# Storing a quarter of two heads through GpSimd's DMA queue

## The chip, the cores and the metric

The kernel runs on one core of a Trainium2 chip. The core has compute engines (PE for matmuls, VectorE or DVE, ScalarE or ACT, GpSimd or POOL), a queue engine SP, and 16 DMA engines that move data between HBM (the chip's DRAM) and SBUF (on-chip memory with 128 partitions). [...] DMAs are issued by SP, ACT or GpSimd; each issuer has a queue of its own, and all queues run on the same 16 DMA engines. The metric is device time in microseconds (us); lower is better.

## The reference

```python
# q, k: (8, 12, 1024, 64) float32
def reference(q, k):
    return np.einsum('bhid,bhjd->bhij', q, k).astype(np.float32)
```

For each of the 96 heads a 1024 x 64 matrix is multiplied with the transpose of another: 1024 x 1024 scores of 4 bytes, 4 MB for a head, 402.65 MB written in all, against 50.33 MB read.

## The kernel before, in words

The 96 heads are worked in blocks of 2, 2, 4, 8, 8 and then six times 12. Inputs of a block are loaded by `load` (L66, ACT's queue from the second load on), cast to fp16 by GpSimd (L127), and transposed by VectorE (L145) into `qT` and `kT`. This runs a block or two ahead; in the last block, heads 84 to 95, nothing is left to load, cast or transpose.

`scores` (L156) makes one head. PE multiplies (L171) into PSUM in four pieces of 128 x 2048; ScalarE copies each piece into the head's output tile `o_sb` (L181); then SP issues one store of the whole tile (L185). In `o_sb` a partition holds eight rows of the head's result (index t, 0 to 7), each 1024 floats, and partition p holds rows 8p to 8p + 7; so what one partition stores is one run of 32 KB in HBM, and the head is 128 such runs.

`out_pool` (L45) has three buffers. The first copy into `o_sb` for head n + 3 therefore waits for the store of head n to land, all of it. All instructions are held in the order in which they are written (`pin`), on each engine; what runs when is decided by that order and by the waits on semaphores.

A DMA reports its end through a semaphore, to which the DMA engines that took part add their marks. The kernel's DMAs take their semaphores in turn out of eight for each kind of queue, so a DMA also waits for the landing of the one that stood eight before it.

Of the kernel before, what the change touches and what calls it, by code (L numbers as in the profile page):

```python
# [10 lines left out]
P = 128  # L11

@with_exitstack
def kernel(
# [6 lines left out]
    nc = tc.nc  # L21

    B, H, S, D = q.shape
    NT = S // P
    BH = B * H
# [5 lines left out]
    of = out.rearrange("b h i j -> (b h) i j")  # L31
# [3 lines left out]
    PE_BLOCKS = 2  # L35
    NMAX = max(sizes)
    CHUNK = 48 * 32

    consts = ctx.enter_context(tc.tile_pool(name="consts", bufs=1))
    ident = consts.tile([P, P], F16)  # L40
# [4 lines left out]
    out_pool = ctx.enter_context(tc.tile_pool(name="out_pool", bufs=3))  # L45

    pin = tc.keep_in_program_order

    def half_tile():
        half_sb = half_pool.tile([P, CHUNK], F16, tag="half")  # L50
        return half_sb

    class Block:
# [3 lines left out]
        def __init__(self, first, N, by_pe):  # L57
# [5 lines left out]
            self.halves = {}  # L63
            self.cut = max(1, self.R * 32 // CHUNK + (self.R * 32 % CHUNK > 0))

# [90 lines left out]
        def scores(self, n, side, ps_pool, w):  # L156

            half, g = divmod(n, self.N // 2)
            cs = slice(half * D, (half + 1) * D)

            qT = self.qT.rearrange("c (g m t) -> c g t m", t=NT, m=P)
            kT = self.kT.rearrange("c (g j) -> c g j", j=S)
            o_sb = out_pool.tile([P, NT, S], F32, tag="out")
            for u in range(NT // w):
                ps = ps_pool.tile([P, w * S], F32, tag="po")
                for tt in range(w):
                    for j in range(2):
                        js = slice(j * 512, (j + 1) * 512)
                        at = tt * S + j * 512
                        pin(  # L170
                            nc.tensor.matmul(  # L171
                                ps[:, at : at + 512],
                                qT[cs, g, w * u + tt],
                                kT[cs, g, js],
                            )
                        )
                dst = o_sb[:, w * u : w * u + w].rearrange("p t j -> p (t j)")
                if w == 1 and u % 2:
                    pin(nc.vector.tensor_copy(out=dst, in_=ps))  # L179
                else:  # L180
                    pin(nc.scalar.copy(out=dst, in_=ps))  # L181
                for do in side.get(u, []):
                    do()
            pin(
                nc.sync.dma_start(  # L185
                    out=of[self.first + n].rearrange("(p t) j -> p (t j)", p=P),
                    in_=o_sb.rearrange("p t j -> p (t j)"),
                )
            )

    blocks, first = [], 0
    for i, N in enumerate(sizes):
# [5 lines left out]
    at = 0  # L198
# [110 lines left out]
```

## Time and profile before

| | |
|---|---|
| median of three runs | 1063.38 us (1062.9 to 1063.62) |
| span of the profiled execution, first to last instruction | 1061.8 us |
| HBM traffic over the span | 427 GB/s |
| stores, issue to landing, median of 96 | 21.8 us |
| copies PSUM to `o_sb`, L181 (ScalarE) | 695.3 us in 384 instructions, mean 1.86 us |
| ScalarE waiting for a store to land | 298.4 us |
| DMA instructions of GpSimd | none |

Only the span is given for the profiled execution; the median of the runs is 1.6 us above it, and that difference lies before its first and behind its last instruction. A busy time is the time in which an engine had an instruction at work. "DMA share" is the mean busy share of the 16 DMA engines. In the chain of waits, each line names what was waited for, with its start and duration. An engine name with a q (SPq, ACTq) is the queue side, where DMAs are issued.

### The profile page before, as it was taken

Reading aid. Unit: us, or ns where it says so; the run is one execution under the profiler, and the core shown is the slowest. Engines: PE = TensorE matmul, PEld = TensorE weight load, DVE = VectorE, ACT = ScalarE, POOL = GpSimd, SP = SyncE. Lnnn points to the kernel's source line nnn. Section 1 sums busy time; section 2 is a strip of 40 time slices with the busy share of each in tenths; the row PEclk is TensorE's granted clock in tenths of the full one; section 3 lists DMA queues with packets and bytes.
Section 4 is the critical chain, followed back from the end, with each engine's and each line's share of the span. In section 5 each row is a group of like instructions: output and inputs, shape, how many; then the busy total and the mean of one; then the engine's idle time right before and its main releaser. Section 6 shows DMA issues by size and latency. Waiting matters only on the chain.

```text
span 1061.8 us, 4282 instructions
## 1 busy us (share of the span) xinstructions
PE 701.3 (66%) x1568; PEld 241.6 (23%) x1568; DVE 471.5 (44%) x75; ACT 697.6 (66%) x386; POOL 368.3 (35%) x286
## 2 busy tenths in 40 slices
PE   6866755755677367773677836777367777778770
PEld 2322211211222122221222212222122222222220
DVE  2999601991696007960079600795007950000000
ACT  4856745755777366774677746777467777777771
POOL 6959128607630463303733046330463200000000
DMA  9999999999999999999999999999999999999997
GB/s 385 428 429 435 433 431 435 435 422 440 428 430 432 432 430 432 435 422 429 431 433 431 415 436 431 433 435 422 428 434 435 434 432 432 434 433 427 434 431 311
DMA packets 17588, 453.25 MB, mean 427 GB/s; under 512 B 1952, under 2 KB 1952, under 8 KB 2976
## 3 DMA queue, kind: packets, MB, share of 16 engines
q1 hardware_dynamic: 14688, 406.85, 89.1%
q10 hardware_dynamic: 2880, 46.14, 10.4%
q8 instruction: 12, 0.20, 0.1%
q14 instruction: 8, 0.07, 0.0%
HBM read 50.33 MB, written 402.65 MB: 427 GB/s over the span
## 4 chain that ended last, share of the span: by engine, by line
DMA 70%; ACT 17%; PE 7%; DVE 2%; issue 1%; POOL 1%; ACTq 0%; SPq 0%
DMA out_dram<-o_sb 70%; ACT o_sb L181 17%; PE ps L171 7%; DVE qT L145 1%; DVE kT L145 1%; DMA early<-in_q_dram 0%; POOL half_sb L127 0%; PE ps L151 0%; POOL half_sb L97 0%; DVE kT L154 0%; DVE o_sb L179 0%; ACTq L181 0%; ACT kT L154 0%; SPq L84 0%; ACTq L73 0%
## 5 line engine op out<-in xcount | busy, mean ns | idle before, releaser
L181 ACT COPY o_sb<-ps 128x2048 f32<-128x2048 f32 (+1 forms) x384 | 695.3, 1860 | 334.7 <-DMA out_dram<-o_sb 298.4
L171 PE MATMUL ps<-kT,qT 64*128 64x512 f16 x1536 | 697.2, 617 | 329.4 <-ACT o_sb L181 325.6
L127 POOL CAST half_sb<-x_sb 32x1536 f16<-32x1536 f32 (+1 forms) x256 | 346.5, 1353 | 455.1 <-DMA x_sb<-in_q_dram 318.3
L171 PEld LDWEIGHTS <-qT 64*128 64x128 f16 x1536 | 238.4, 157 | 786.3 <-issue 781.9
L145 DVE STREAM_TRANSPOSE qT<-half_sb 128x1536 f16<-128x1536 f16 (+1 forms) x34 | 232.8, 7140 | 372.2 <-issue 372.2
L145 DVE STREAM_TRANSPOSE kT<-half_sb 128x1536 f16<-128x1536 f16 (+1 forms) x34 | 234.2, 7181 | 0.0
L127 POOL CAST half_sb<-early 32x1024 f16<-32x1024 f32 x16 | 16.5, 1033 | 4.0 <-DMA early<-in_q_dram 3.3
L151 PE MATMUL ps<-ident,half_sb 128*128 128x128 f16 x32 | 4.1, 309 | 6.7 <-POOL half_sb L97 6.1
L154 DVE COPY qT<-ps 128x1024 f16<-128x1024 f16 x2 | 2.4, 1224 | 12.3 <-PE ps L151 12.3
L179 DVE COPY o_sb<-ps 128x1024 f32<-128x1024 f32 x4 | 4.9, 1224 | 4.3 <-PE ps L171 4.3
L97 POOL CAST half_sb<-early 128x512 f16<-128x512 f32 x8 | 4.6, 613 | 4.1 <-DMA early<-in_q_dram 4.1
L151 PEld LDWEIGHTS <-half_sb 128*128 128x128 f16 x32 | 3.2, 139 | 8.6 <-POOL half_sb L97 6.5
L154 ACT ACT_TABLE_LOAD x1 | 1.3, 1283 | 5.8 <-DMA early<-in_q_dram 5.8
L154 DVE COPY kT<-ps 128x1024 f16<-128x1024 f16 x1 | 1.2, 1224 | 4.3 <-PE ps L151 4.3
L154 ACT COPY kT<-ps 128x1024 f16<-128x1024 f16 x1 | 1.0, 1012 | 1.2 <-PE ps L151 1.2
masks.py:199 POOL TENSOR_SCALAR_AFFINE_SELECT ident<-ident 128x128 f16<-128x128 f16 x1 | 0.3, 292 | 0.1
masks.py:197 POOL MEMSET ident<- 128x128 f16 x1 | 0.2, 204 | 0.3 <-POOLq L293 0.3
L293 POOL MEMSET const-float32-0.0<- 128x1 f32 x1 | 0.1, 98 | 0.2 <-issue 0.2
L293 POOL MEMSET const-uint8-127<- 128x1 uint8 x1 | 0.1, 101 | 0.0
L293 POOL MEMSET const-bfloat16-1.0<- 128x1 bf16 x1 | 0.1, 100 | 0.0
L293 POOL MEMSET const-float32-1.0<- 128x1 f32 x1 | 0.1, 98 | 0.0
## 6 DMA issues: line engine op xcount, KB each, us to landing
out_dram<-o_sb SPq DMA_DIRECT2D x96, 4096.0 KB, 21.8
x_sb<-in_q_dram ACTq DMA_DIRECT2D x6, 3072.0 KB, 22.8
x_sb<-in_k_dram ACTq DMA_DIRECT2D x6, 3072.0 KB, 39.6
x_sb<-in_k_dram ACTq DMA_DIRECT2D x2, 2048.0 KB, 22.2
x_sb<-in_q_dram SPq DMA_DIRECT2D x1, 2048.0 KB, 18.0
x_sb<-in_q_dram ACTq DMA_DIRECT2D x1, 2048.0 KB, 19.0
early<-in_k_dram ACTq DMA_DIRECT2D x4, 256.0 KB, 5.0
early<-in_q_dram SPq DMA_DIRECT2D x4, 256.0 KB, 4.7
```

What stands on the lines that cost most here:

```text
L97: nc.gpsimd.tensor_copy(out=self.rows[x][:, :, half], in_=self.raw[x][:, half * n : (half + 1) * n].rearrange("p (r d) -> p r d", d=D),)
L127: nc.gpsimd.tensor_copy(out=half_sb[q0 : q0 + 32].rearrange("p (r d) -> p r d", d=32), in_=raw[32 * b : 32 * b + 32, c * m : (c + 1) * m, h],)
L145: pin(nc.vector.transpose(out=dst, in_=src))
L151: pin(nc.tensor.transpose(t_ps[:, t], self.rows[x][:, t], ident))
L154: pin(copy(out=dst, in_=src))
L171: nc.tensor.matmul(ps[:, at : at + 512], qT[cs, g, w * u + tt], kT[cs, g, js],)
L179: pin(nc.vector.tensor_copy(out=dst, in_=ps))
L181: pin(nc.scalar.copy(out=dst, in_=ps))
L293: nc = _bacc.Bacc("TRN2", target_bir_lowering=False, num_devices=1)
```

## The change

Heads 86 and 90 (`BH - 10` and `BH - 6`) are stored otherwise; all others as before. Of these two heads, rows t = 0 to 4 and t = 6 of every partition are stored by SP, in two DMAs. Rows t = 5 and t = 7 (two runs of 4 KB per partition) are stored by GpSimd for partitions 0 to 125, in nine DMAs of 14 partitions each: partitions r, r + 9, r + 18 and so on. Behind each of the nine stands a thin DMA that stores 32 columns of the same two rows for partitions 126 and 127. In head 86 four more thin DMAs stand ahead of the first of the nine. The columns of partitions 126 and 127 that the thin DMAs leave over are stored by SP, in one DMA. GpSimd thus issues 22 DMAs for head 86 and 18 for head 90, SP three for each.

```diff
+    SHIFTED = (BH - 10, BH - 6)
...
+    def store_head(head, dst, src):
+        if head not in SHIFTED:
+            store(
+                nc.sync,
+                dst.rearrange("p t j -> p (t j)"),
+                src.rearrange("p t j -> p (t j)"),
+            )
+            return
+        def part(eng, rows, cols):
+            store(eng, dst[rows, 5:8:2, cols], src[rows, 5:8:2, cols])
+
+        for t in (slice(0, 5), slice(6, 7)):
+            store(
+                nc.sync,
+                dst[:, t].rearrange("p t j -> p (t j)"),
+                src[:, t].rearrange("p t j -> p (t j)"),
+            )
+        last, w, at = slice(126, 128), 32, 0
+        begin = 4 if head == SHIFTED[0] else 0
+        part(nc.sync, last, slice((begin + 9) * w, S))
+        for i in range(begin + 9):
+            if i >= begin:
+                r = i - begin
+                part(nc.gpsimd, slice(r, r + 9 * 13 + 1, 9), slice(0, S))
+            part(nc.gpsimd, last, slice(i * w, (i + 1) * w))
...
-            pin(
-                nc.sync.dma_start(
-                    out=of[self.first + n].rearrange("(p t) j -> p (t j)", p=P),
-                    in_=o_sb.rearrange("p t j -> p (t j)"),
-                )
-            )
+            dst = of[self.first + n].rearrange("(p t) j -> p t j", p=P)
+            store_head(self.first + n, dst, o_sb)
```

In the built program the first copy into the buffer for head 89, and for head 93, waits on the semaphores of GpSimd's DMAs as well as on SP's. From its ninth DMA on, each DMA of GpSimd waits for the landing of the one eight before it.

More of the change, by code (lines that the diff above doesn't have):

```diff
@@ L47, with store @@
     pin = tc.keep_in_program_order
+    def store(eng, dst, src):
+        pin(eng.dma_start(out=dst, in_=src))
+    def store_head(head, dst, src):
[22 more added lines that the diff above has]
+            part(nc.gpsimd, last, slice(i * w, (i + 1) * w))
     def half_tile():
```

## The prediction

> **What bounds the kernel now.** I read the page first: busy times, then the DMA rows, then the chain.
>
> ```profile
> PE 701.3 (66%) x1568; PEld 241.6 (23%) x1568; DVE 471.5 (44%) x75; ACT 697.6 (66%) x386; POOL 368.3 (35%) x286
> DMA  9999999999999999999999999999999999999997
> q1 hardware_dynamic: 14688, 406.85, 89.1%
> DMA 70%; ACT 17%; PE 7%; DVE 2%; issue 1%; POOL 1%; ACTq 0%; SPq 0%
> ```
>
> No compute engine is above 66%, while the 16 DMA engines are full in every slice but the last, and 70% of the chain is the store `out_dram<-o_sb`. Bytes only move earlier or later; what an edit can win is idle time of single DMA engines at the end. So the second look is the tail, in windows (the last two columns are the mean share of the 16 engines that is busy, and GB/s):
>
> ```profile
> 1050.00:1052.00 2.00, 0.00 (x0) 0.00 (x0) 0.00 (x0) 0.00 (x0) 0.00 (x0) 1.00 1.10 475
> 1052.00:1054.00 2.00, 0.00 (x0) 0.00 (x0) 0.00 (x0) 0.00 (x0) 0.00 (x0) 1.00 0.76 328
> 1054.00:1056.00 2.00, 0.00 (x0) 0.00 (x0) 0.00 (x0) 0.00 (x0) 0.00 (x0) 1.00 0.27 115
> 1056.00:1058.00 2.00, 0.00 (x0) 0.00 (x0) 0.00 (x0) 0.00 (x0) 0.00 (x0) 1.00 0.08 33
> 1058.00:1060.00 2.00, 0.00 (x0) 0.00 (x0) 0.00 (x0) 0.00 (x0) 0.00 (x0) 1.00 0.04 16
> ```
>
> Most engines are done by 1055; one of sixteen (0.06) works on to 1060. The trace keeps one completion mark for each engine of a store, without the engine's name. For the last store they come at 1052.82, then thirteen from 1054.08 to 1056.26, one at 1057.06, one at 1060.86. That last one is a laggard with a history: it falls back by 0.10 us in nearly every store (7.0 us behind the first at 875, 8.0 at 1002), its 32 KB rows taking 1.216 to 1.236 us where 1.213 is the median. So the end is set by one DMA engine, 3.8 us behind the next.
>
> The third look is the chain near the change:
>
> ```profile
> 951.33 21.77 DMA out_dram<-o_sb
> 973.20 1.87 ACT o_sb L181
> 975.12 1.88 PE ps L171 x4
> 977.02 3.64 ACT o_sb L181 x2
> 980.68 21.76 DMA out_dram<-o_sb
> ```
>
> The store of head 86 goes out at 951.33; its landing releases the buffer for head 89, whose copies take 7.5 us and whose store goes out at 980.68. There are three buffers, so a store that lands late delays the store three heads on.
>
> **The change, part by part.** Heads 86 and 90 are changed; both lie in the last block, where VectorE and GpSimd have nothing else (DVE ends near 876), so no work is queued behind GpSimd's new DMAs.
>
> *Bytes by engine.* Prices of one row in the trace's DMA records: 32 KB 1.213 us, 24 KB 0.912, 16 KB 0.611, 8 KB 0.309, 2 KB 0.084, a mark 0.009. Between them 20 KB is 0.76 and 4 KB 0.16. A normal store is 8 rows of 32 KB on each engine: 9.70 us. A changed head keeps on SP's queue 8 rows of 20 KB and 8 of 4 KB: 8 x 0.76 + 8 x 0.16 = 7.36. GpSimd's nine DMAs of 14 partitions add, if 14 engines take one partition each, 9 x 2 x 0.16 = 2.9 and nine marks (0.1): 10.35, or 0.6 more than now. The two engines left out carry 7.36 and some 128-byte pieces (nine times two, under 0.084 each by the 2 KB row, so 0.3 to 1.5; nearest is a bare overhead like the mark's, I take 0.3): 7.7, or 2.0 less. SP's thin leftover (2 rows of 2.4 to 2.9 KB on two engines) is 0.2 at most. Over two heads: 4.1 us off a pair of engines, 1.2 us onto the other fourteen.
>
> *Which pair.* 14 + 2 is 16, so if shares go round the engines in turn, every DMA of 14 meets the same pair left out, and the four thin DMAs ahead in head 86 turn the pair by eight. No row of the trace names the laggard, and GpSimd issues no DMA in it. If the laggard is in the pair, it ends at 1060.86 - 4.1 = 1056.8; the next engine ends at 1057.06 + 1.2 = 1058.3, and that is the new end: 2.6 us gained. If it is not, the end is 1060.86 + 1.2 = 1062.1. [...]
>
> *Issue on SP.* Three DMAs for one: 0.33 us each (332 ns), 0.7 us more, beside a queue that is 12 us deep. Nothing.
>
> *Issue on GpSimd, the wait and its cover.* Head 86 needs 22 of its DMAs, head 90 18, each waiting for the landing of the one eight before. The first copy of head 89 (and of 93) now waits for all of them; behind that copy stand the remaining copies on ScalarE, then PE's PSUM, then SP's stores. What covers a late landing is the queue: store 85's marks come at 955.5 to 963.3, behind them lie 7.36 + 2 x 9.71 + 3.0 = 29.8 us of work, so the first engine runs dry at 985, the second-latest (959.5) at 989.3, a relieved laggard at 963.3 + 7.4 + 19.5 + 0.3 = 990.5. Store 89 reaches the engines 7.5 us of copies and 1 to 2 of issue after the release. So a release by about 980, 28.7 us after issue (now 21.8), costs nothing at the end, and each later microsecond costs one.
>
> How long will 22 DMAs take? Issue: between SP's 0.33 and the 1.20 of ACT's 3 MB load, 7 to 26 us. Turns: where loads share the engines with stores, rows of the two queues alternate one for one:
>
> ```profile
> 467.25 33.51 DMA out_dram<-o_sb
> ...
> x_sb<-in_k_dram ACTq DMA_DIRECT2D x6, 3072.0 KB, 39.6
> ```
>
> Two loads of 8 rows per engine need 16 x (0.91 + 1.21) = 34 us and the lag, which is the 39.6; the store beside them took 33.5. So each turn of GpSimd's queue waits for a 1.21 us row. With one turn per DMA it needs 10 x 1.21 + 3 = 15 us on an engine; with one per 4 KB row 20 turns, 27 us; with one for the mark too (as the loads' marks show in the records) 30 turns, 39 us, cut short when the store queue runs dry. The limit of 28.7 lies inside. I take 20 turns, 27 us, issue hidden behind them: between the ends, and nearest to what a row of its own costs. Then nothing is lost.
>
> **Sum.** Span 1061.8 minus 2.6 is 1059.2. The runs' median, 1063.38, lies 1.6 us above the profiled span (start and end of the program); the same 1.6 gives 1060.8 us, 0.24% faster. About 0.2% (2.1 us) is what a measurement of this kernel can tell from no change.
>
> **Rivals.**
> *Late release (slower).* Marks take turns of their own, or GpSimd's issue is near 1.2 us. The release comes when the store queue runs dry, near 987 to 991; store 89 reaches the engines at 996 to 1000, a hole of 6 to 10 us behind the second-latest engine's 989.3, part of which the laggard's relief gives back. Head 90 does it again, with 18 DMAs and less queue. One small hole nets +3 (1066), two full ones about +17 (1080); the middle, 1070. It decides from a release of head 86 later than 980. For it: the marks' own turns in the load phases. Against it: GpSimd's pieces are small and idle engines pass them at 0.16 us each.
> *Marks from all engines.* If each GpSimd DMA posts a mark on all 16 engines, the thirteen thin ones add 13 turns: 40 turns instead of 30, or 22 even at one turn per DMA, 27 us and more. It lands in the same hole, at 1065 to 1080. [...]
> *Wrong pair.* Shares fall so that the laggard is among the fourteen, or the DMAs spread over all: end 1062.1, time 1064.6 (+0.1%), and not below 1063.4.
> *Both late engines in the pair.* The third, 1056.26 + 1.2 = 1057.5, sets the end: 1060.0.
>
> **How the numbers follow.** Forecast 0.45 (own range 1059.8 to 1062), late release 0.25, marks from all engines 0.12, wrong pair 0.13, both in the pair 0.05. The forecast lies 0.5 us inside the bound, so a quarter of it counts as no change; so do most of the wrong pair and the mildest late releases. Faster: 0.45 x 0.77 + 0.05 = 0.40. Slower: 0.25 + 0.12 and a little of the wrong pair, 0.39. Same: 0.21. Range: 1059.6 (both engines) to 1073, past the middle of the late case, leaving out its two full holes and a tip below, about 0.15.
>
> **What will show it.** In the chain, the store of head 86 should land within 29 us of its issue and that of 90 likewise; DMA share in windows stays near 1.0 from 980 to 1050; the last marks of the last store lie within 3 us instead of 8. A wrong pair shows as a last mark alone by 3 us or more and later than 1060.9. A late release shows as ScalarE waiting far more than 2.3 us before the first copy of head 89 or 93, and a slice with DMA share under 0.8 behind it. The prediction is wrong if the span grows, or if the laggard is relieved and the end does not move: then another engine's work, not the release, was mis-sized.

## The result and the profile after

The changed kernel takes 1088.58 us (1087.98 to 1089.27) against 1063.48: ratio 1.0238, interval 1.0226 to 1.0250, so 25.1 us slower where 2.6 us less was forecast. Its profiled execution spans 1086.6 us, 24.8 more than before.

The page after, the lines that answer to those of before, with GpSimd's queue as a new line (software_dynamic) and the groups' new line:

```profile
PE 700.9 (65%) x1568; PEld 241.7 (22%) x1568; DVE 471.4 (43%) x75; ACT 697.1 (64%) x386; POOL 390.9 (36%) x326
DMA  9999999999999999999999999999999999995969
q1 hardware_dynamic: 14988, 404.78, 86.9%
q0 software_dynamic: 1568, 2.08, 0.7%
DMA 70%; ACT 18%; PE 9%; issue 1%; POOL 0%; DVE 0%; ACTq 0%; SPq 0%; POOLq 0%
L51 POOL DMA_DIRECT2D out_dram<-o_sb x40 | 22.6, 565 | 181.5 <-ACT o_sb L211 145.7
```

Busy times of the compute engines are as before. GpSimd moves 2.08 MB of 453 and needs 0.565 us to issue a DMA; neither looks like 25 us. But the DMA row, full to the end before, has two slices with holes. In windows (the last two columns are the DMA share and GB/s):

```profile
980.00:990.00 10.00, 0.00 (x0) 0.00 (x0) 0.00 (x0) 0.00 (x0) 1.13 (x2) 1.00 0.91 364
990.00:1000.00 10.00, 2.79 (x7) 1.11 (x8) 0.00 (x0) 4.52 (x3) 0.00 (x0) 1.00 0.07 26
1000.00:1010.00 10.00, 9.40 (x22) 3.03 (x20) 0.00 (x0) 9.60 (x6) 0.00 (x0) 1.00 0.74 315
...
1040.00:1050.00 10.00, 1.22 (x3) 0.46 (x3) 0.00 (x0) 3.14 (x2) 0.00 (x0) 1.00 0.41 160
1050.00:1060.00 10.00, 9.59 (x22) 3.30 (x21) 0.00 (x0) 9.42 (x6) 0.00 (x0) 1.00 0.49 210
```

Missing shares times length: 0.9 + 9.3 + 2.6 = 12.8 us in the first hole, 5.9 + 5.1 = 11.0 in the second. In both ScalarE starts to copy again only after the engines have run dry. The chain of waits says for what:

```profile
951.45 2.91 POOL out_dram L51 x5
954.36 14.59 DMA out_dram<-o_sb
968.94 0.28 issue
969.23 14.42 DMA out_dram<-o_sb
983.65 0.28 issue
983.93 10.88 DMA out_dram<-o_sb
994.82 0.02 issue
```

The three DMA pieces are links of GpSimd's DMAs, each waiting for the landing of the one eight before. The last lands at 994.8, 43.4 us after GpSimd issued its first DMA for head 86; only then may head 89 be copied. Before, that release came 21.8 us after the issue of the store. Head 90's comes at 1046.5, 36 us after its first DMA. And this is why its queue crawls (DMA queues in the window 970 to 986, packets first):

```profile
q1 hardware_dynamic: 217, 6.23, 92.5%
q0 software_dynamic: 215, 0.36, 8.7%
```

One packet of GpSimd for one of SP's, while SP's are rows of up to 32 KB and GpSimd's carry next to nothing. It is so for the whole stretch: from 956.5 to 987.5 us the trace has 591 records of each of the two queues. So here a record of GpSimd takes a turn, in which it waits for one record of SP's. By size, the 1568 records of GpSimd's queue are 504 rows of 4 KB (18 x 28), 44 of 256 bytes (the thin DMAs' data), 640 marks (40 x 16) and 380 more of 8 or 4 bytes, which are 22 x 14 + 18 x 4. The records name no engine, but the counts fit if a DMA of GpSimd puts records on all 16, empty ones where it has no data, and a mark on each, also on those that move nothing. Then a DMA of 14 partitions takes three turns on every engine and a thin one two: 9 x 3 + 13 x 2 = 53 turns for head 86, 45 for head 90.

The sums: since 951 us an engine has on average 109.6 us of work in the records, before 103.6, and idles 26.0 us, before 7.2. So 18.8 us of the 24.8 are idle time and 6.0 are work. Of the 6.0, 4.0 are rows that took longer than the same size takes undisturbed; about 1.0 is 0.44 MB that in the kernel before had gone out by 951 us; the rest is smaller rows, marks and empty records. The two holes (23.8 us) cost less than their size, because they let the laggard catch up: the last store's marks lie within 0.85 us, before within 8.05.

### The profile page after: what moved, and what is told of

It reads as the page before. It is cut to its first block, busy times and chain, and to the rows that moved or that the text cites. A ratio compares the mean times of both kernels' runs of the same rounds, so it can differ in the third digit from the quotient of the medians.

```text
span 1086.6 us, 4343 instructions
## 1 busy us (share of the span) xinstructions
PE 700.9 (65%) x1568; PEld 241.7 (22%) x1568; DVE 471.4 (43%) x75; ACT 697.1 (64%) x386; POOL 390.9 (36%) x326
## 3 DMA queue, kind: packets, MB, share of 16 engines
q0 software_dynamic: 1568, 2.08, 0.7%
## 4 chain that ended last, share of the span: by engine, by line
DMA 70%; ACT 18%; PE 9%; issue 1%; POOL 0%; DVE 0%; ACTq 0%; SPq 0%; POOLq 0%
DMA out_dram<-o_sb 70%; ACT o_sb L211 18%; PE ps L201 9%; DMA early<-in_q_dram 0%; POOL out_dram L51 0%; PE ps L181 0%; POOL half_sb L127 0%; ACTq L211 0%; DVE kT L184 0%; DVE o_sb L209 0%; ACT kT L184 0%; SPq L114 0%; POOLq L330 0%
## 5 line engine op out<-in xcount | busy, mean ns | idle before, releaser
L51 POOL DMA_DIRECT2D out_dram<-o_sb x40 | 22.6, 565 | 181.5 <-ACT o_sb L211 145.7
## 6 DMA issues: line engine op xcount, KB each, us to landing
out_dram<-o_sb SPq DMA_DIRECT2D x94, 4096.0 KB, 21.8
```

What stands on the lines that cost most here:

```text
L51: pin(eng.dma_start(out=dst, in_=src))
```

## The experiments

Theory A: the loss is the late release, from GpSimd's turns. B: the small packets cost the engines the time themselves. C: the wait for the DMA eight before. Later D (rows stretch when a DMA's engines read partitions that other engines read) against E (small DMAs are dear wherever they read). Times of before beside them were 1063.05 to 1063.41 us (medians of each set). The diffs are against the changed kernel and show the main lines alone; where a `part` line is added, it stands in the place of SP's leftover DMA and all of GpSimd's DMAs.

**Release without GpSimd.** The two rows go to a tile of their own (a free input buffer, by two copies of 1024 columns for each of the last two of 2048), so `o_sb` waits for SP's stores alone.

```diff
-            store(eng, dst[rows, 5:8:2, cols], src[rows, 5:8:2, cols])
+            store(eng, dst[rows, 5:8:2, cols], two[rows, :, cols])
...
+                    pin(nc.scalar.copy(out=o_sb[:, 2 * u], in_=ps[:, :S]))
+                    pin(nc.scalar.copy(out=two[:, u - 2], in_=ps[:, S:]))
```

> The two rows that GpSimd stores are copied to a tile of their own, so the output tile of heads 86 and 90 is released by SP's stores alone; the 40 DMAs of GpSimd stay. Theory A (the loss is the late release: the copies of heads 89 and 93 wait for GpSimd's DMAs, which crawl because each takes turns with 32 KB store rows on all 16 engines): both holes close, 1060 to 1066 us, ScalarE waits about 2.3 us before heads 89 and 93. Theory B (the small rows, pads and marks cost the DMA engines themselves the 25 us): still 1080 us or more.

1068.72 us, ratio 1.0054 (1.0039 to 1.0069). The chain has nearly the old rhythm again, store to release in 21.6 us for head 86 and 24.8 for head 89 (21.8 before):

```profile
950.50 21.55 DMA out_dram<-o_sb
972.16 1.88 ACT o_sb L217
979.64 24.83 DMA out_dram<-o_sb
```

All 40 DMAs are still there, and 19.9 us are gone. The engines have 109.9 us of work since 951 us, as in the change, but idle 6.1 instead of 26.0. That much is the wait, as A says; B is out as the main cause. But 5.7 us stay without any hole, and the time lies 2.7 us above what A allowed.

**The other pair.** As that one, without the four thin DMAs ahead. The cursor of the expectation is the engine at which the next share would start; that shares go round the engines so is an assumption of the author's, and no record shows it.

```diff
-        begin = 4 if head == SHIFTED[0] else 0
+        begin = 0
```

> As the spare-tile kernel, without the four thin DMAs ahead in head 86, so the pair of engines that the DMAs of 14 leave out is another one, if a cursor moves by 14 and by 2. If the slow engine of the kernel before is in the pair left out with the four thin DMAs, this kernel is 2 to 4 us slower than the spare-tile kernel; if it is in the other pair, 2 to 4 us faster; if in neither, or if there is no such pair, equal within 1 us.

1068.17 us, ratio 1.0045 (1.0030 to 1.0060), not told apart from 1068.72. So neither pair, if there are two, is worth more than the other.

**One DMA of 126.** GpSimd's bytes in two DMAs per head, `o_sb` released by all as in the change.

```diff
+        part(nc.gpsimd, slice(0, 126), slice(0, S))
+        part(nc.gpsimd, slice(126, 128), slice(0, S))
```

> The same bytes from GpSimd in two DMAs per head, one of 126 partitions and one of two, in the output tile as in the change. Theory A by turns: 18 rows and 2 marks and a thin row are some 22 turns per engine where the change has 53 and 45, so the release comes some 29 us after issue where it was 43 and 36: 1062 to 1068 us. Theory C (not the turns but the wait of each DMA for the one eight before makes it late): no such wait is left, so 1062 to 1064 us, with landing under 27 us. Theory B: 1080 us or more.

1067.5 us, ratio 1.0039 (1.0025 to 1.0054); the store is released 24.3 us after issue (951.24 to 975.54). The time lies where A had it, above what C had. The release does not: A had it some 29 us after issue, C under 27. So this run does not tell A from C, and the 4 us left are no hole.

**The same split on SP.**

```diff
+        part(nc.sync, slice(0, 126), slice(0, S))
+        part(nc.sync, slice(126, 128), slice(0, S))
```

> The same split, 126 and 2 partitions, issued by SP in the queue of the stores: no second queue, so no turns. Theories A and C: no hole, 1062 to 1065 us; below 1062 only if the slow engine is one of the two that a DMA of 126 partitions leaves out on this queue. Theory B (small rows as such are dear): several us slower, as 4 KB rows stand here too.

1071.61 us, ratio 1.0079 (1.0064 to 1.0094): 8.6 us lost without GpSimd, and without turns. A and C had said at most 1065, so neither accounts for it. In the records the 4 KB rows of SP's queue take 216 ns on average (the median is 159) and 32 KB rows beside them 1235 (1217 before). The count of small records (260 from 940 to 1072 us) fits 14 marks for each DMA of 126 partitions, so 14 engines, with nine partitions each if the shares are equal. This gave theory D.

**All 128 partitions, on SP and on GpSimd.**

```diff
+        part(nc.sync, slice(0, 128), slice(0, S))
```

> As the split on SP, but the two rows go out in one DMA of all 128 partitions, eight per engine as in a whole store. Theory D (rows are stretched where a DMA's engines read partitions that another engine reads in the other stores: 126 partitions are nine per engine): the 4 KB rows fall back to 0.16 us, the summed stretch of all rows since 951 us from about 4.8 us per engine to under 1, time within 2 us of the kernel before. Theory E (4 KB rows from three DMAs per head are dear wherever they come from): still 4 us or more above.

> GpSimd stores the two rows in one DMA of 128 partitions per head. Turns: 16 rows and a mark on each engine, 17 x 1.21 + 2.6 = 23 us and the start of some 5 us, so the release comes about 26 to 29 us after issue. Theory D: no stretch, no hole that shows at the end: 1063 to 1066 us. Theory E: 1067 us or more, as with the DMA of 126 partitions (1067.5).

On SP 1064.05 us, ratio 1.0006 (0.9996 to 1.0015); on GpSimd (the same line with `nc.gpsimd`) 1064.24, ratio 1.0009 (0.9999 to 1.0018). The stretch, which is the time of all rows since 951 us above what 4, 20 and 32 KB take undisturbed (0.159, 0.76 and 1.213 us), falls from 4.8 us per engine to 0.7 and 0.8 (0.3 before); 4 KB rows take 161 and 160 ns. E is out for this size: the same rows from three DMAs per head are all but free, from either queue. GpSimd's one DMA needs 17 turns (544 records for 2 x 16), and head 86 is released after 21.9 us, sooner than the 26 to 29 expected.

**Same DMAs, other partitions.** Four DMAs of 32 partitions on SP, first every fourth partition, then 32 neighbours.

```diff
+        for r in range(4):
+            part(nc.sync, slice(r, r + 125, 4), slice(0, S))
...
+            part(nc.sync, slice(32 * r, 32 * r + 32), slice(0, S))
```

> The two rows in four DMAs of 32 partitions on SP's queue, partitions r, r + 4, r + 8 and so on: two partitions per engine, on all 16, taken from the same eight partitions as in a whole store if that gives engine i partitions 8i to 8i + 7. Theory D (the stretch comes from reading another engine's partitions): 4 KB rows at 0.16 us, within 2 us of the kernel before. Theory E (many small DMAs are dear as such): 3 us or more above, like the next.

> [...] Theory D: rows stretch as with 126 partitions or more (four engines read the same eight partitions), several us above the kernel of stride 4. Theory E: the same time as that.

Every fourth: 1064.5 us, ratio 1.0010 (1.0000 to 1.0019). Neighbours: 1071.66, ratio 1.0077 (1.0060 to 1.0094). Rows, sizes, counts and queue are the same, and in both runs the ten DMAs more than before leave 16 marks each (2112 records under 512 bytes, before 1952). Windows behind the two stores, every fourth first:

```profile
965.00:975.00 10.00, 7.26 (x17) 2.52 (x17) 0.00 (x0) 7.43 (x6) 0.00 (x0) 1.00 1.07 451
1000.00:1010.00 10.00, 7.51 (x18) 2.65 (x17) 0.00 (x0) 7.29 (x5) 0.00 (x0) 1.00 1.03 431
```

and neighbours:

```profile
965.00:975.00 10.00, 7.26 (x16) 2.50 (x16) 0.00 (x0) 5.45 (x4) 0.00 (x0) 1.00 1.05 357
1000.00:1010.00 10.00, 7.46 (x18) 2.69 (x17) 0.00 (x0) 7.46 (x5) 0.00 (x0) 1.00 1.00 358
```

The engines are as busy (share 1.0), but move 357 GB/s instead of 451: a row occupies its engine for longer. That is what D forecast. The 4 KB rows take 239 ns against 161, the stretch is 5.4 us per engine against 0.5. Of the 7.0 us between the two spans, 4.1 are work of the engines and 3.0 idle time. A rival for this pair is that 32 neighbours lie close together; it does not cover the split on SP, where 126 of all 128 partitions stretch nearly as much (216 ns). So in these runs the choice of partitions decides. Why it does stays open: which engine reads which partition stands in no record, and D needs the condition in the expectation, that engine i of a whole store reads partitions 8i to 8i + 7; for its four engines on the same eight partitions it needs besides that each of the 16 takes two neighbours of the 32. Neither is shown. With the partitions, the places in HBM that are written at the same time change too, and no run separates the two.

**Which engine is slow.** Tiny DMAs of k partitions behind the last store, on SP, which leave k marks each; 64 columns of the last head's row 7 are otherwise left out.

```diff
+        for i, k in enumerate((4, 7, 8, 12, 14, 15)):
+            at = S - 64 + 8 * i
+            store(nc.sync, dst[:k, 7, at : at + 8], src[:k, 7, at : at + 8])
```

> The stores of the kernel before; of the last head the last 64 columns of row 7 are left out but for six DMAs of 4, 7, 8, 12, 14 and 15 partitions behind the last store, 8 columns each. If a DMA of k partitions on SP's queue runs on the first k engines, the times of its k marks name the engines that finish late: the last mark of the last store stands alone by 3 us, and appears among the marks of those k alone that take the slow engine in. If it appears first with 8, the slow engine is number 7; if with none, number 15; first with 15, number 14. Time within 2 us of the kernel before.

With k = 4 the marks come at 1053.84, 1054.49, 1055.53 and 1056.48; with 7 there are three more, one of them at 1060.72, behind the next of that DMA by 4.1 us. So, if k partitions run on the first k engines, the slow engine is not among the first four, but among the first seven: none of the numbers 7, 14 and 15 that the expectation names. The kernel took 1064.11 us in one run. With other k:

> As the kernel with marks by engine (the same 64 columns of the last head's row 7 left out), with DMAs of 5, 6, 7, 8, 14 and 15 partitions. The late mark was absent with 4 and present with 7, so the slow engine is the fifth, sixth or seventh of the queue's order: its mark, alone by 3 us, appears first with 5, with 6 or with 7.

The late mark (1060.46) is there with k = 5; absent from the first four in the run before, it is by the same condition the fifth, number 4 from 0 (1064.04 us, one run). It is not alone this time: two engines among numbers 8 to 13 end only 0.2 and 0.7 us earlier, so the 3.8 us by which the next one was ahead in the profile of before does not hold in every execution. That k partitions run on the first k engines is an assumption of the author's, as no record names an engine; the k marks per DMA and the nested times agree with it.

> The spare-tile kernel, with the same marks behind the last store (64 columns of the last head's row 7 left out). If the pair that GpSimd's DMAs of 14 leave out is engines 6 and 7 (counted from 0), those two end several us ahead of the others, and the slow engine, if it is one of them, is no longer last. If moving rows between DMA engines does not relieve the one left out (because the rows it used to read are still read through the same way by others), the slow engine is last as before.

One run, 1071.32 us. By the same condition the fifth engine is still last, 1067.28, the next at 1062.69. Compared with the marks kernel just above, number 4 ends 7.0 us later, number 5 7.2, number 6 5.3 and number 7 2.7. So the slow engine is not relieved. Of 6 and 7, the pair that the expectation names, only 7 stands out, by 3 to 4 us where the sum had 5.3 (4.1 off, 1.2 on the others); whether 6 was its partner, one run does not settle.

**The thin DMAs alone.** The change without them; SP stores partitions 126 and 127.

```diff
+        part(nc.sync, slice(126, 128), slice(0, S))
+        for r in range(9):
+            part(nc.gpsimd, slice(r, r + 9 * 13 + 1, 9), slice(0, S))
```

> The change without its 22 thin DMAs: SP stores partitions 126 and 127 whole, GpSimd keeps the nine DMAs of 14 per head in the output tile. The thin ones carry 18 KB together. Theory A by turns: 27 turns per engine and head instead of 53 and 45; from the first packet near 956 that is some 4 us of store 85, the 16 short rows of head 86 (7.4 us), some eight rows of store 87 (9.7 us) and 4.4 us of GpSimd's own rows, so the release falls to 981 to 985 and the holes to 0 to 5 us each; with the stretch of some 5 us the time is 1067 to 1073 us. If the thin DMAs are as cheap as their bytes, the release stays near 994 and the time above 1083 us.

1066.84 us, ratio 1.0033 (1.0020 to 1.0046), 0.2 us under the range. Turns fall to 27 per head (864 records for 2 x 16), the releases to 978.0 (27.0 us after GpSimd's first DMA, before the 981 expected) and 1021.1 (27.5 us), and the holes are gone:

```profile
980.00:990.00 10.00, 9.54 (x22) 3.24 (x22) 0.00 (x0) 9.43 (x7) 0.00 (x0) 1.00 1.01 436
990.00:1000.00 10.00, 9.40 (x22) 3.19 (x21) 0.00 (x0) 9.59 (x6) 4.39 (x8) 1.00 0.97 401
1025.00:1035.00 10.00, 9.42 (x22) 3.29 (x21) 0.00 (x0) 9.47 (x6) 0.00 (x0) 1.00 0.97 416
```

So 22 DMAs that move 11 KB (44 records of 256 bytes; the 18 KB of the expectation is too much) cost 21.7 us of the 25.1. No run tests C on its own, since fewer DMAs also wait less. Against it stands the count of the changed kernel, 591 records to 591 up to 987.5 us: by this count GpSimd's queue had a packet ready for every turn, although its DMAs waited for the one eight before.

No version beat the kernel before; the best, 1064.05, is the same within its interval.

## Why the prediction was wrong, by its steps

- **Bound, cover and limit: held, as far as two releases show.** The limit was put at about 980. At 978.0 (no thin DMAs) there is no hole; at 994.8 there is one of 12.8 us of mean engine time. The late rivals had the release at 987 to 991 and 6 to 10 us for the hole.
- **"I take 20 turns, 27 us": the step that failed.** The DMAs of 14 were counted at two turns and the thin ones at next to none. They take three and two, 53 in all, and the release came after 43.4 us. (Not each turn cost 1.21 us: head 86's own rows are shorter, and from 987.5 us on SP's queue was running dry, with 9 rows of 32 KB in 2.5 us on 16 engines.) The load phase had shown marks with turns of their own, and the text named that row and then chose a lower value. The rival "Late release", given 0.25, had these turns of the marks. "Marks from all engines", given 0.12, comes nearest to the mechanism; its 40 turns missed the 13 records that the thin DMAs leave ahead of their marks, and its 1065 to 1080 missed the stretch and a second hole nearly as deep as the first. Its condition, a mark on all 16 engines for each of GpSimd's DMAs, fits the records of the changed kernel: 640 marks for 40 DMAs.
- **"4 KB is 0.16": right for a row left alone, wrong here.** The rows of GpSimd's DMAs took 0.209 us on average in the changed kernel, and stretched the 32 KB rows beside them from 1.217 to 1.239. 4.0 us per engine were in no term of the sum and no rival.
- **"Which pair": here too the sum failed, and the rival "Wrong pair" held in its premise.** No run shows that each DMA of 14 leaves out the same pair, so the 4.1 us off two engines, and the 2.6 us gained, stand on an assumption. In their place the runs showed a slow engine that is number 4, if k partitions run on the first k engines, and that in the one run of the spare-tile kernel with marks was not relieved: it ended at 1067.28, with the next at 1062.69. The rival's 1064.6 lacked the stretch: with a prompt release the time was 1068.72 with the four thin DMAs ahead and 1068.17 without them, so nothing was gained.
- **Issue on GpSimd: in its bounds** (0.565 us, between 0.33 and 1.20), but its first packet reached an engine at 956.55, 5.1 us after issue, a start that the 27 us left out.
- **Signs to look for: right.** The landing past 29 us, ScalarE's long wait (24.3 us, where 2.3 was normal) and the DMA share under 0.8 behind it are what the trace shows.

## What to carry to other kernels

Price a DMA on a second queue in turns, not bytes: here it waited on every engine behind one row of the busy queue for each piece, mark and empty record, up to 1.2 us each, and 22 DMAs with 53 such turns landed after 43.4 us. Ask at once whose buffer it holds. And when a transfer is split over partitions, measure the split: here all 128, or every fourth, left the rows of 4 KB at 160 or 161 ns, while 126 (216 ns), every ninth (209) or 32 neighbours (239) stretched them. The busy share here did not tell stretched rows from others (1.05 and 1.00 against 1.07 and 1.03); GB/s did (357 and 358 against 451 and 431).

## What the hardware showed that was not expected

- The DMAs of GpSimd left 4 or 8 byte records beside their data and marks, as many as fit the engines for which they had no data: 380 in the changed kernel, 128 with DMAs of 126 and 2 partitions, none with DMAs of 128.
- 4 KB rows took 239 ns instead of 161 by the choice of partitions (and, with it, of the places in HBM), at the same number and size of rows.
- The laggard was number 4 of 16 in SP's order, counted from 0, if k partitions run on the first k engines; behind the next it was by 3.5, 0.2 and 4.6 us in the three kernels with marks.
- The second hole levelled the engines: behind it the 16 marks of store 93 came within 0.18 us.
